# Gate projections in block products of four, rotary tables on another engine, and a reordered merge, in a hybrid diffusion layer

## The chip, the cores and the metric

The kernel runs on one core of one Trainium2 chip. The core has a matrix engine (PE, with its weight loads shown as PEld), a vector engine (DVE), an activation engine (ACT), a general engine (POOL) and a queue engine that issues most transfers (SP). The metric is the device time of one execution in microseconds (us); a lower time is better. Times are medians of several runs; the profile is one more execution, taken by the hardware profiler.

## The reference

One layer over 1024 latent tokens of width 1024 with 256 context tokens. Cut to what matters:

```python
m_lat = (silu(c) @ w_mod + b_mod).reshape(1, 1, 6, 1024)           # modulation rows
h_lat = rms_norm(x, norm_mix) * (1 + m_lat[:, :, 1]) + m_lat[:, :, 0]
aq, ak, av, bq, bk, bv, cq, cf, cb, ci, cg, gates = features(h_lat, w_in, ...)  # h_lat @ w_in, norms, rotary
yc = hgrn2_bidir(cq, cf, cb, ci, cg, ...)          # branch 2, linear recurrence in both directions
ya = window_attn(aq, ak, av, ctx k, ctx v, sink)   # branch 0, 8 heads, 2 key heads
yb = global_attn(bq, bk, bv, ctx k, ctx v)         # branch 1
up = einsum('blnw,nwd->blnd', stack(ya, yb, yc), w_branch)
x_mix = x + m_lat[:, :, 2] * (sum_n(sigmoid(gates) * up) @ w_out)
h = rms_norm(x_mix, norm_ffn) * (1 + m_lat[:, :, 4]) + m_lat[:, :, 3]
x = x_mix + m_lat[:, :, 5] * conv_ffn(h, ...)
return rms_norm(x, norm_final)
```

The gates are 3072 of the input projection's columns: for each of three branches eight tiles of 128 channels, 24 gate tiles in all.

## The kernel before

All products run with each fp32 operand split into a high part (a cast by ACT) and a low part (the difference, by DVE), and three matmuls for each pair: high by high, high by low, low by high. Everything lies with 128 partitions; the hidden state is `hh`, `hl`, each 128 x 8 x 1024.

The stages follow each other in this order: modulation rows 0 and 1, context and norm; the HGRN branch by four heads (`hgrn_head`); the stage between (lines 628 to 850); window attention (branch 0) and global attention (branch 1), both through `attention`; the merge (`merge_up`) and output projection (`wo_half`); the ConvFFN.

The framework places the instructions of each engine by a simulated run: an instruction has a priority from its place in the program, `tc.high_priority(offset=n)` moves it n places ahead, and among what is ready the first goes. Each engine then works through its own list in order, SP's list of transfers too. A tile comes from a pool with a fixed number of buffers for each tag; a new tile waits until a buffer of that tag is released.

The 24 gate tiles are listed in `gates` (line 612) as pairs (branch, tile) in the branch order 2, 0, 1. Before the change they are computed in four ways:

- `gates[0]` fills gaps of the last HGRN head (line 622), `gates[1:4]` are plain (`plain_gates`, line 689). A plain gate (`gate_unit`, line 564) takes 2 halves x 8 k x 3 = 48 matmuls of 512 columns; each half is drained by ACT (line 580) and stored by SP (line 581).
- `gates[4:10]` go in three pairs (`gate_pair`, line 738) through the scheme in `pair` (line 697): a 2 x 2 block product with seven multiplications in place of eight. One block side is the weights of two units by halves of the contraction, the other the hidden state by halves of the contraction and of the tokens.
- `gates[10:17]` are filler for the matrix engine in the first attention and `gates[17:24]` in the second (lines 853 to 859); `attention` spreads their steps over its iterations.

The block products need four sums of hidden-state blocks, T1 to T4 (`ht`, made by `h_sums`, line 654): DVE adds high and low parts into whole tiles (line 661), subtracts them (line 666), ACT casts and DVE takes the difference (lines 633 and 634). In the program these sums are woven with the three plain gates (line 693). `ctile` gives the tiles with tag "c", five buffers, for whole sums and for results. Product q uses block S_ORDER[q] (line 695): (0,0), T1, T2, (1,1), T3, (1,0), T4. Its weights come from one or two loads, a DVE sum (line 711) and a split (`w_split`), at a priority 100 places ahead; the results are drained by ACT copies or DVE sums.

The token projections (q, k, v of both attentions) go through the same scheme in three pairs (`tok_pair`, line 803). They use two two-bank tiles in PSUM, `za` and `zb`, in turn, and two single banks for product 5. A gate pair uses the two banks of one tile in turn and one single bank. After a token pair's product its results get a head norm (for branch 1) and the rotary step; these pieces wait in the list `behind`, and after every region of a later product one piece is put in. The rotary tables `tbq` and `tbk` are made once by POOL (line 684).

Token pairs and gate pairs alternate (lines 846 to 848).

In `attention` the result of an iteration is stored to `y_d` by SP (line 1640), each store after the iteration's last DVE operation.

`merge_up` (line 1751) goes through the branches in the order 2, 0, 1. For each it loads four tiles y from `y_d` (line 1761), splits them (lines 1762 and 1763), and multiplies by eight tiles of `w_branch`; a gate tile is loaded, put through a sigmoid and multiplied on. Before each gate tile it takes one step of `mod_rest` (line 588), which computes the modulation rows 2 and 3: a step loads 128 rows of `w_mod` into the only buffer `wmr` and DVE adds them, scaled, onto `macc`. There are 18 steps and 24 places, so they start with the first tile of the first branch.

Of the kernel before, what the change touches and what calls it, by code (L numbers as in the profile page):

```python
# [18 lines left out]
P = 128  # L19
D = 1024  # L20
KT = D // P
L = 1024
# [24 lines left out]
SPRIO = 40  # L47
TILED = 2
# [37 lines left out]
def build(tc, ins, out):  # L86
    nc = tc.nc
    V, A, G, T, SP = nc.vector, nc.scalar, nc.gpsimd, nc.tensor, nc.sync
    with ExitStack() as top:
# [522 lines left out]
        gates = [(n, i) for n in (2, 0, 1) for i in range(KT)]  # L612

# [30 lines left out]
        with ExitStack() as sp3:  # L644
# [9 lines left out]
            def h_sums():  # L654

                for k in range(0, KQ, 2):
                    ks = slice(k, k + 2)
                    f = {}
                    for a, b in ((0, 0), (0, 1), (1, 1), (1, 0)):
                        f[a, b] = ctile(f"h{a}{b}{k}")  # L660
                        V.tensor_tensor(out=f[a, b], in0=hb[a, b][0][:, ks].bitcast(F32),
                                        in1=hb[a, b][1][:, ks].bitcast(F32), op=add_)
                        yield

                    def put(n, out, x, y):
                        V.tensor_tensor(out=out, in0=x, in1=y, op=sub)
                        split([p[:, ks] for p in ht[n]], out)

                    put(1, f[0, 0], f[0, 1], f[0, 0])
                    yield  # L670
                    put(3, f[0, 1], f[1, 1], f[0, 1])
                    yield
                    put(2, f[1, 1], f[1, 1], f[0, 0])
                    yield
                    put(4, f[1, 0], f[1, 0], f[1, 1])
                    yield

# [3 lines left out]
            for nm, g in (("q", qnb), ("k", knb)):  # L681
                tb = p3.tile([P, LT, 2, 2, 32], F32, tag=f"tb{nm}", name=f"tb{nm}", bufs=1)
                for r in range(2):
                    G.tensor_tensor(out=tb[:, :, :, r], in0=cs,
                                    in1=g[:, None, None, r * 32:(r + 1) * 32].to_broadcast([P, LT, 2, 32]),
                                    op=ALU.mult)
                tabs[nm] = tb

            def plain_gates():
                for n, i in gates[1:4]:  # L690
                    yield from gate_unit(p3, n, i, "mm", ctile(f"g{n}{i}"))

            weave((plain_gates(), 48), (h_sums(), 16))

            S_ORDER = ((0, 0), 1, 2, (1, 1), 3, (1, 0), 4)

            def pair(nm, W, n, regions, unit, drains, behind):

                def load(t, i, j):
                    SP.dma_start(t, W(i, j))  # L700
                    return t

                def raw(i, j):
                    cnt[0] += 1
                    t = wp.tile([P, 1024], F32, tag="wr", name=f"wr{cnt[0]}", bufs=WR)[:, :KQ * n]
                    return load(t.rearrange("p (k n) -> p k n", k=KQ), i, j)

                s = p3.tile([P, 1024], F32, tag="s", name=f"s{nm}", bufs=1)[:, :KQ * n].rearrange("p (k n) -> p k n", k=KQ)
# [5 lines left out]
                for q in range(7):  # L714
                    with tc.high_priority(offset=wprio[0] + SPRIO):
# [13 lines left out]
                        w = w_split(src, KQ, n)  # L729
                    b = S_ORDER[q]  # L730
                    h = hb[b] if isinstance(b, tuple) else ht[b]
                    for x in range(len(regions(q))):
                        unit(regions(q)[x], w, h, x, q in (0, 1, 5))
                        for _ in range(1 if behind else 0):
                            behind.pop(0)()
                    drains(q)

            def gate_pair(g0, g1):

                nm = f"{g0[0]}{g0[1]}"  # L740
                idx = [U_C["gate"] + g[0] * 8 + g[1] for g in (g0, g1)]
                z = mm2(f"gp{nm}")
                zb = bank("b", f"gpb{nm}", (P, 512))
                cA, cB = ctile(f"gA{nm}"), ctile(f"gB{nm}")
                zq = lambda q: zb if q == 5 else z[:, q % 2 if q < 4 else 0]

                def unit(z, w, h, x, new):
                    wh, wl = w
                    hh_, hl_ = h
                    for k in (2 * x, 2 * x + 1):  # L750
                        on = dict(skip_group_check=True)
                        T.matmul(z, wh[:, k], hh_[:, k], start=new and k == 0, stop=False, **on)
                        T.matmul(z, wh[:, k], hl_[:, k], start=False, stop=False, **on)
# [1115 lines left out]
```

## Time and profile before

| | us |
|---|---|
| median of 3 runs | 2103.16 (2102.41 to 2103.4) |
| the profiled execution, device time | 2104.95 |
| its span, first to last instruction | 2103.2 |
| PE busy in it | 2028.2 |
| mean granted clock of PE, as a share of full | 0.99 |

A row of the timeline gives the start in us, the duration of one instruction (or of a row of them, with their count at the end), the engine, the line, the operation, output<-inputs by tile names, and in brackets how long the engine stood idle before it and what it waited for. A row of waits gives the waiting engine, tile and line, what it waited for, the sum in us, how many times, and the longest. A row of windows gives, for a stretch, the busy time and the count of each engine, the granted clock, the DMA share and GB/s. Durations of matmuls overlap, so their cost is read from start to start.

### The profile page before, as it was taken

What the parts mean: (1) busy time and instruction counts of PE and PEld (TensorE: products, weight loads), DVE (VectorE), ACT (ScalarE), POOL (GpSimd) and SP (SyncE); (2) the same over time, 40 slices, a digit from 0 to 9 for tenths busy, and PEclk for the clock granted to TensorE, in tenths of its full rate; (3) what the DMA queues carried; (4) which work ended last, traced back from release to release, by engine and by line L of the source; (5) the groups of instructions that cost most, each with busy time, mean ns of one, the idle gap of its engine ahead of it and who ended that gap; (6) DMA issues with size and microseconds to landing.
All of it is one profiled execution on the core that took longest, in us unless ns stands there. A gap on an engine that the chain in (4) does not pass through costs nothing. (4 is left out here: it accounts for less than half of the span.)

```text
span 2103.2 us, 29756 instructions
## 1 busy us (share of the span) xinstructions
PE 2028.2 (96%) x11321; PEld 1684.1 (80%) x11321; DVE 1521.3 (72%) x2440; ACT 1037.1 (49%) x1770; POOL 274.0 (13%) x245
## 2 busy tenths in 40 slices
PE   8999999989998999999999799999999999999997
PEld 5888888878996788788888577888888888888886
DVE  4846656686757788578887667888877777779964
ACT  3433333332233877688888633446445445544442
POOL 0000000021002232100000000010332343300001
PEclk9999999999999999999999999999999999999999
DMA  9311111133445211210110286592222222258722
GB/s 369 134 45 34 38 51 41 41 100 118 140 130 173 84 48 53 89 40 32 36 33 29 75 271 226 182 310 92 93 87 83 78 87 83 81 211 313 267 69 81
DMA packets 105023, 239.19 MB, mean 114 GB/s; under 512 B 10288, under 2 KB 35248, under 8 KB 103856
## 3 DMA queue, kind: packets, MB, share of 16 engines
q1 hardware_dynamic: 104880, 237.29, 33.8%
q8 instruction: 89, 1.46, 0.3%
q14 instruction: 54, 0.44, 0.1%
HBM read 191.64 MB, written 45.61 MB: 113 GB/s over the span
## 5 line engine op out<-in xcount | busy, mean ns | idle before, releaser
L1622 DVE TENSOR_TENSOR pl<-pp,ph 128x512 fp32r<-128x512 f32 x236 | 159.5, 687 | 31.8 <-ACT ph L1621 26.3
L166 ACT CAST wh<-wr 128x1024 fp32r<-128x1024 f32 x73 | 76.7, 1051 | 196.9 <-PE wo L191 34.4
L167 DVE TENSOR_TENSOR wl<-wr,wh 128x1024 fp32r<-128x1024 f32 x73 | 91.6, 1254 | 84.9 <-ACT wh L166 83.4
L1621 ACT CAST ph<-pp 128x512 fp32r<-128x512 f32 x236 | 135.6, 585 | 34.7 <-PE pp L1617 32.1
L190 PE MATMUL gz<-hh,wh 128*128 128x512 f32 x288 | 117.8, 410 | 8.4 <-ACT cg L580 6.9
L1209 PE MATMUL dn<-ac,wh 128*128 128x512 f32 (+2 forms) x311 | 119.3, 384 | 1.3 <-DVE xt L1217 1.2
L1210 PE MATMUL dn<-ac,wh 128*128 128x512 f32 (+2 forms) x311 | 119.3, 383 | 0.5 <-DVE ac L634 0.5
L1211 PE MATMUL dn<-ac,wl 128*128 128x512 f32 (+2 forms) x311 | 119.2, 383 | 0.0
L192 PE MATMUL gz<-hh,wl 128*128 128x512 f32 x288 | 114.9, 399 | 1.1 <-DVE wl L167 1.1
L191 PE MATMUL gz<-hl,wh 128*128 128x512 f32 x288 | 114.7, 398 | 0.0
L1603 PE MATMUL po<-ph,VHL 128*128 128x512 f32 x236 | 106.1, 450 | 1.9 <-ACT ph L1621 1.3
L1604 PE MATMUL po<-pl,VHL 128*128 128x512 f32 x236 | 97.9, 415 | 0.3 <-DVE pl L1622 0.2
L190 PE MATMUL br<-yh,wh 128*128 128x512 f32 x192 | 76.3, 399 | 11.2 <-ACT yh L1762 11.0
L191 PE MATMUL br<-yl,wh 128*128 128x512 f32 x192 | 76.5, 399 | 2.0 <-DVE yl L1763 1.9
L633 ACT CAST wh<-wr 128x1024 fp32r<-128x1024 f32 (+1 forms) x42 | 37.6, 897 | 82.2 <-PE tmt L826 22.5
L1617 PE MATMUL pp<-ident,plat 128*128 128x128 f32 x512 | 76.6, 273 | 0.3 <-DVE pl L1622 0.2
L1617 PEld LDWEIGHTS pp<-ident,plat 128*128 128x128 f32 x512 | 62.5, 140 | 17.6 <-DVE pl L1622 2.3
L956 ACT ACTIVATE u<-c,cw 128x1024 f32<-128x1024 f32 x38 | 47.3, 1246 | 58.0 <-DVE c L1111 30.0
L192 PE MATMUL br<-yh,wl 128*128 128x512 f32 x192 | 75.6, 395 | 0.0
L634 DVE TENSOR_TENSOR wl<-wr,wh 128x1024 fp32r<-128x1024 f32 (+1 forms) x42 | 43.1, 1029 | 44.7 <-ACT wh L633 44.7
L190 PEld LDWEIGHTS gz<-hh,wh 128*128 128x128 f32 x288 | 54.9, 191 | 18.0 <-ACT cg L580 7.6
L1209 PEld LDWEIGHTS dn<-ac,wh 128*128 128x128 f32 x311 | 58.4, 188 | 13.1 <-DVE xt L1217 1.0
(1531 smaller groups left out, 6316.6 us busy)
## 6 DMA issues: line engine op xcount, KB each, us to landing
wr<-in_w_up SPq DMA_DIRECT2D x44, 512.0 KB, 3.6
wr<-in_w_cm SPq DMA_DIRECT2D x42, 512.0 KB, 3.7
wmr<-in_w_mod SPq DMA_DIRECT2D x32, 512.0 KB, 5.0
wr<-in_w_dn SPq DMA_DIRECT2D x30, 512.0 KB, 4.3
b<-act_d SPq DMA_DIRECT2D x25, 512.0 KB, 5.8
sgt<-gate_d SPq DMA_DIRECT2D x24, 512.0 KB, 4.6
wr<-in_w_tm SPq DMA_DIRECT2D x23, 512.0 KB, 3.7
act_d<-u SPq DMA_DIRECT2D x22, 512.0 KB, 2.6
```

The lines of the kernel that those rows point to most:

```text
L167: (lo_eng or V).tensor_tensor(out=lo[:, :n], in0=raw[:, :n], in1=hi[:, :n].bitcast(F32), op=ALU.subtract)
L190: T.matmul(psl, wh[:, k, c], hh[:, k0 + k, cols], start=s, stop=False)
L191: T.matmul(psl, wh[:, k, c], hl[:, k0 + k, cols], start=False, stop=False)
L192: T.matmul(psl, wl[:, k, c], hh[:, k0 + k, cols], start=False, stop=e)
L1209: T.matmul(z, w[0][:, c], h[0], start=s, stop=False, **on)
L1210: T.matmul(z, w[0][:, c], h[1], start=False, stop=False, **on)
L1211: T.matmul(z, w[1][:, c], h[0], start=False, stop=e, **on)
L1603: T.matmul(po, vv, ph, start=n == 0, stop=False)
L1604: T.matmul(po, vv, pl, start=False, stop=n == len(kts) - 1)
L1617: T.transpose(pp[:, h], PT(h, n), ident)
L1621: A.copy(ph, pp)
L1622: V.tensor_tensor(out=pl, in0=pp, in1=ph.bitcast(F32), op=ALU.subtract)
```

## The change

It changes five things.

1. `gates.insert(2, gates.pop())` moves the last gate, (1, 7), to place 2. Two gates, `gates[1]` and `gates[2]`, are plain. Eight, `gates[3:11]`, go in two groups of four (`gate_group`), each after a token pair; the first two token pairs follow each other. The attentions have 7 and 6 gates as filler.
2. A group's weights are two gates side by side, so a tile is 128 x 4 x 256 and comes by two transfers of 256 KB whose pieces are 512 bytes. A group uses two two-bank tiles in turn and two single banks, 24 matmuls of 512 columns a product. Up to four pieces of `behind` are put in after each product of either kind.
3. `h_sums` comes in the program behind both plain gates, all of T1 first, and the rotary tables behind it, made by DVE.
4. The modulation steps are left out of the first branch of the merge; the tiles 0 and 4 of the other two take two steps. The loads and splits of the first branch's y get priority `YPRIO` = 100.
5. The last two stores of the second attention go through POOL's queue.

```diff
+YPRIO = 100
...
         gates = [(n, i) for n in (2, 0, 1) for i in range(KT)]
+        gates.insert(2, gates.pop())
...
+                def whole(a, b, k):
+                    f[a, b, k] = ctile(f"h{a}{b}{k}")
...
                 for k in range(0, KQ, 2):
...
+                    whole(0, 0, k)
+                    whole(0, 1, k)
+                    t = f[0, 0, k]
+                    put(1, t, f[0, 1, k], t, k)
+                for k in range(0, KQ, 2):
+                    b, t = f[0, 1, k], f[0, 0, k]
+                    whole(1, 1, k)
+                    put(3, b, f[1, 1, k], b, k)
+                    put(2, t, f[1, 1, k], t, k)
+                    whole(1, 0, k)
+                    put(4, t, f[1, 0, k], t, k)
+            for x in (1, 2):
+                for _ in gate_unit(p3, *gates[x], "mm", ctile(f"g{x}")):
+                    pass
+            h_sums()
...
-                    G.tensor_tensor(out=tb[:, :, :, r], in0=cs,
+                    V.tensor_tensor(out=tb[:, :, :, r], in0=cs,
...
-            weave((plain_gates(), 48), (h_sums(), 16))
...
                 def load(t, i, j):
-                    SP.dma_start(t, W(i, j))
+                    ws = W(i, j)
+                    n = 256 // len(ws)
+                    for x, w in enumerate(ws):
+                        SP.dma_start(t[:, :, x * n:(x + 1) * n], w)
                     return t
...
-                        for _ in range(1 if behind else 0):
-                            behind.pop(0)()
+                        for _ in range(4 // len(regions(q))):
+                            if behind:
+                                behind.pop(0)()
...
-            def gate_pair(g0, g1):
+            def gate_group(gs):
...
+                z = [mm2(f"{nm}{x}") for x in range(2)]
...
+                def regions(q):
+                    if q == 5:
+                        if not zc:
+                            zc.extend(bank("ab"[x], f"{nm}c{x}", (P, 512)) for x in range(2))
+                        return zc
+                    z_ = z[q % 2 if q < 4 else 0]
+                    return [z_[:, x] for x in range(2)]
                 def unit(z, w, h, x, new):
...
+                    cs_ = slice(x * P, (x + 1) * P)
+                    for k in range(KQ):
+                        T.matmul(z, w[0][:, k, cs_], h[0][:, k], start=new and k == 0, stop=False, **on)
+                        T.matmul(z, w[0][:, k, cs_], h[1][:, k], start=False, stop=False, **on)
+                        T.matmul(z, w[1][:, k, cs_], h[0][:, k], start=False, stop=k == KQ - 1, **on)
...
+                    if q >= 3:
+                        n, i = gs[(int(x[0]) - 1) * 2]
+                        SP.dma_start(gate_d[n, i:i + 2, :, (t1, t2)[int(x[1]) - 1]].rearrange("i p t -> p i t"), c[x])
...
-            for x, (a, b) in enumerate((((0, 2), (1, 2)), ((0, 0), (0, 1)), ((1, 0), (1, 1)))):
-                tok_pair(a, b)
-                gate_pair(*gates[4 + 2 * x:6 + 2 * x])
+            tok_pair((0, 2), (1, 2))
+            tok_pair((0, 0), (0, 1))
+            gate_group(gates[3:7])
+            tok_pair((1, 0), (1, 1))
+            gate_group(gates[7:11])
...
-        SP.dma_start(y_d[br].rearrange("k p t -> p k t")[:, 2 * g:2 * g + 2, tt * P:(tt + 1) * P], yT)
+        (G if br and it >= n_it - 2 else SP).dma_start(y_d[br].rearrange("k p t -> p k t")[:, 2 * g:2 * g + 2, tt * P:(tt + 1) * P], yT)
...
+            with tc.high_priority(offset=0 if j else YPRIO):
+                y = mp.tile([P, L], F32, tag="y", name=f"y{n}{k}")
+                SP.dma_start(y, y_d[n, k])
+                A.copy(yh[:, 0], y)
+                V.tensor_tensor(out=yl[:, 0], in0=y, in1=yh[:, 0].bitcast(F32), op=ALU.subtract)
...
-                next(mr, None)
+                if j:
+                    next(mr, None)
+                    if i % 4 == 0:
+                        next(mr, None)
```

More of the change, by code (lines that the diff above doesn't have):

```diff
@@ L733, in pair @@
                         unit(regions(q)[x], w, h, x, q in (0, 1, 5))
-                        for _ in range(1 if behind else 0):
-                            behind.pop(0)()
+                        for _ in range(4 // len(regions(q))):
+                            if behind:
+                                behind.pop(0)()
                     drains(q)
-            def gate_pair(g0, g1):
[L740 to L745, printed above, removed]
-                def unit(z, w, h, x, new):
[L748 to L753, printed above, removed]
-                        T.matmul(z, wl[:, k], hh_[:, k], start=False, stop=k == KQ - 1, **on)
@@ L756, in drains @@
                 def drains(q):
[L757 removed]
+                    x = OUT[q]
+                    if x not in c:
+                        c[x] = ctile(f"{nm}{x}")
+                    z_ = z[q % 2 if q < 4 else 0]
                     if q in (0, 1, 2, 6):
[L759 to L762 removed]
@@ L763, in drains @@
-                    if q >= 5:
-                        n, i = (g0, g1)[q - 5]
-                        SP.dma_start(gate_d[n, i], (cA, cB)[q - 5].rearrange("p a b -> p (a b)"))
-                pair(nm, lambda i, j: ins["w_cm"][idx[i]].rearrange("p (k n) -> p k n", n=P)[:, j * KQ:(j + 1) * KQ], P,
-                     lambda q: [zq(q)] * 2, unit, drains, behind)
+                        A.copy(c[x], z_)
+                    elif q == 5:
+                        for y in range(2):
+                            V.tensor_tensor(out=c[x][:, y], in0=zc[y], in1=c[x][:, y], op=add_)
+                    else:
+                        V.tensor_tensor(out=c[x], in0=z_, in1=c[x], op=add_)
@@ L770, in rope, with W @@
+                    if q >= 3:
+                        n, i = gs[(int(x[0]) - 1) * 2]
+                        SP.dma_start(gate_d[n, i:i + 2, :, (t1, t2)[int(x[1]) - 1]].rearrange("i p t -> p i t"), c[x])
+                def W(i, j):
+                    return [ins["w_cm"][U_C["gate"] + n * 8 + g].rearrange("p (k n) -> p k n", n=P)[:, j * KQ:(j + 1) * KQ]
+                            for n, g in gs[2 * i:2 * i + 2]]
+                pair(nm, W, regions, unit, drains, behind)
             def rope(x, nh, tt, tab, nm):
@@ L828, in drains @@
                 def drains(q):
[L829 removed]
+                    x = OUT[q]
                     if x not in c:
```

64 lines of the change are left out of this document (24 added, 40 removed).

## The prediction, made before the changed kernel was run

> **What bounds the kernel now.** I read the head of the page, then the list of PE's waits, then the stages by windows, and last the timelines of the places where PE stands idle.
>
> ```profile
> span 2103.2 us, 29756 instructions
> PE 2028.2 (96%) x11321; PEld 1684.1 (80%) x11321; DVE 1521.3 (72%) x2440; ACT 1037.1 (49%) x1770; POOL 274.0 (13%) x245
> ...
> PE br L190 <- ACT yh L1762: 11.0, 4, 8.9
> PE gp L752 <- ACT cgA L759: 9.9, 4, 4.7
> PE gz L190 <- ACT cg L580: 6.9, 2, 6.8
> PE gp L752 <- ACT cgB L759: 2.7, 3, 1.0
> PE br L191 <- DVE yl L1763: 1.9, 3, 1.1
> PE tmt L824 <- DVE ct L838: 0.3, 1, 0.3
> ```
>
> TensorE bounds it: 2028 of 2103 us. So a change can win in two ways: fewer matmuls, or less of the 75 us in which PE stands. Of those 75 the list puts 12.9 on the first pass of the merge (br), 12.6 on the gate pairs (gp), 6.9 on a plain gate (gz), and only 0.3 on the three token pairs (tmt), which use the same seven products.
>
> ```profile
> 428.90:442.70 13.80, 7.06 (x32) 5.47 (x30) 13.80 (x10) 3.52 (x4) 8.84 (x4) 0.89 0.43 133
> 442.70:461.80 19.10, 18.89 (x78) 15.47 (x79) 19.10 (x18) 7.95 (x10) 0.00 (x0) 0.90 0.24 84
> 501.70:528.40 26.70, 21.67 (x86) 16.43 (x85) 17.80 (x61) 8.49 (x15) 2.75 (x4) 0.94 0.58 177
> 636.00:667.00 31.00, 22.84 (x76) 16.46 (x77) 27.02 (x82) 9.96 (x18) 10.52 (x9) 0.83 0.39 119
> 1195.40:1213.60 18.20, 7.04 (x20) 4.25 (x20) 6.42 (x8) 7.25 (x8) 0.00 (x0) 0.72 0.72 241
> ```
>
> After the length come PE, PEld, DVE, ACT, POOL, then the granted clock. An idle stretch is paid twice: the clock falls to 0.72 to 0.94 around it. The timeline shows both prices:
>
> ```profile
> 443.32 0.63 PE L191 MATMUL gz<-hl,wh 128*128 128x512 f32 x1
> 443.75 0.63 PE L192 MATMUL gz<-hh,wl 128*128 128x512 f32 x1
> ...
> 1341.16 0.39 PE L192 MATMUL br<-yh,wl 128*128 128x512 f32 x1
> ...
> 1346.60 0.39 PE L192 MATMUL br<-yh,wl 128*128 128x512 f32 x1
> ```
>
> A 128x512 matmul costs (1346.60 - 1341.16) / 24 = 0.227 us from start to start (their 0.39 overlaps), and 0.43 (443.32 to 443.75) behind the 6.8 us idle stretch.
>
> **Part 1: matmuls.** A plain gate takes 48 matmuls of 512 columns; a block product of a group of four takes 24, so its seven products take 168, 42 a gate, the same as in the pairs of before (84 for two). Eight gates instead of six in blocks: 2 x 6 x 0.227 = **2.7 us** less. The gate moved to the front costs there what it saves as filler of the second attention.
>
> **Part 2: groups for pairs.** Why pairs stall and token pairs do not:
>
> ```profile
> 508.18 0.79 PE L752 MATMUL gp<-T1h,wh 128*128 128x512 f32 x1 [3.58 <-ACT cgA L759]
> ...
> 501.89 0.62 ACT L633 CAST wh<-s 128x512 fp32r<-128x512 f32 x1 [5.14 <-PE tmt L826]
> 506.63 0.51 ACT L1340 ACTIVATE hsq<-ct 128x128 f32<-128x128 f32 x2 [2.66 <-DVE hrs L1343]
> 507.55 0.57 ACT L759 COPY cgA<-gp 128x512 f32<-128x512 f32 x1
> ```
>
> Product T1 goes to the second bank of the tile that product 0 filled, and PE starts it only after ACT has copied out the first bank (507.55 + 0.57 = 508.1), though its weights were cast at 501.9. ACT is late since it sits in a head norm of the token pair before, which waits for DVE. A pair's product is 12 matmuls, 2.7 us, so nothing covers this. The group takes two separate tiles in turn, as token pairs do; a tile comes round again after a whole other product of 24 x 0.227 = 5.4 us, more than the 3.6 or 4.7 us that ACT is late. So I price it by the token pairs' 0.3, not by the pairs: 12.6 us of waits go, and clock of (1 - 0.94) x 26.7 + (1 - 0.83) x 31.0 = 6.9. Bounds for what is left: 0, and all 19.5. The first products still carry eight rotary steps of the token pair, four per product instead of two; I leave 4 for that: **-15.5 us**. Casts, weight sums and drains get tiles of 1024 instead of 512 and become 14 sets in place of 21; the token pairs run with that size already.
>
> The loads change form: each 512 KB comes as two transfers in 512-byte pieces. The nearest row is a store of such pieces; these lines are the answer for the 3.5 us around one:
>
> ```profile
> DMA packets 272, 0.13 MB, mean 37 GB/s; under 512 B 16, under 2 KB 272, under 8 KB 272
> q1 hardware_dynamic: 272, 0.13, 13.2%
> ...
> wr<-in_w_cm SPq DMA_DIRECT2D x42, 512.0 KB, 3.7
> wr<-in_w_cm SPq DMA_DIRECT2D x21, 256.0 KB, 2.8
> q1 hardware_dynamic: 104880, 237.29, 33.8%
> ```
>
> 0.132 x 16 x 3.5 / 272 = 27 ns a packet; 1024 pieces on 16 engines take 1.7 us. Eight loads per seven products leave 5.4 x 7 / 8 = 4.8 us for each, so nothing waits: 0. The other end is the whole run's mean packet, 0.338 x 16 x 2103.2 / 104880 = 108 ns (rival 4). A load has a fixed part: 512 KB lands in 3.7 us and 256 KB in 2.8, which leaves 1.9 that doesn't shrink. If the two halves stood one behind the other, a load would take 5.6 instead of the 4.8 us there is for it, 16 x 0.8 = 13 us more. [...] I take 0, since both halves are issued together and well ahead, so that their fixed parts can overlap.
>
> **Part 3: sums and tables.** Why the plain gate stalled:
>
> ```profile
> 428.91 4.62 DVE L661 TENSOR_TENSOR ch<-hh,hl 128x1024 f32<-128x1024 f32 x4
> 437.90 2.28 DVE L666 TENSOR_TENSOR ch<-ch,ch 128x1024 f32<-128x1024 f32 x1
> ...
> 432.46 4.43 POOL L684 TENSOR_TENSOR tbq<-cs,qnb 128x512 f32<-128x512 f32 x2 [5.75 <-DMA cs<-in_rope]
> ...
> L824 PE MATMUL tmt<-wh,T2h x48: 283/283/283, 472.9 to 608.4; 128*128 128x256 f32 x48
> ...
> 497.85 0.28 PE L825 MATMUL tmt<-wl,T4h 128*128 128x256 f32 x1
> 497.97 0.28 PE L826 MATMUL tmt<-wh,T4l 128*128 128x256 f32 x1
> ```
>
> While POOL makes the tables a DVE sum takes 2.28 instead of 1.14 us (4.62 / 4). DVE fell behind, ACT's cast of a sum waited, and the gate's drain stood behind that cast. On DVE the four tables, half as long as a sum, cost some 4 x 0.6 = 2.4 us, off PE's path, and ahead of the rotary steps that need them by two products. With both gates ahead of the sums the 6.8 us wait goes, and (1 - 0.90) x 19.1 = 1.9 of clock: 8.7. What is late next is T2. PE came to its product at 472.9; one plain gate less (10.9) and 8.7 less bring that to 453.3. DVE starts at 428.9 and has 21 sum steps and about 6 weight steps ahead of T2's last part: 27 x 1.14 = 30.8, so 459.7, or some 464 if the sums wait for a "c" tile (five tiles, two of them held by the gates until stored). That gap of 6 to 11 us can be filled: the product (1,1) needs no sum and lasts 48 x 0.12 = 5.8 (497.85 to 497.97 is one of its size). I take 5 us of it as left (ends 0 and 11, plus about 2 of clock): **-4 us**.
>
> **Part 4: start of the merge.**
>
> ```profile
> 1179.93 0.39 PE L192 MATMUL gz<-hh,wl 128*128 128x512 f32 x1
> 1194.99 0.49 PE L1604 MATMUL po<-pl,VHL 128*128 128x512 f32 x1 [0.23 <-DVE pl L1622]
> 1204.37 1.22 PE L190 MATMUL br<-yh,wh 128*128 128x512 f32 x2 [8.89 <-ACT yh L1762]
> ...
> 1186.14 11.92 SPq L1640 DMA_DIRECT2D y_d<-yT  x2
> 1198.16 0.91 SPq L1761 DMA_DIRECT2D y<-y_d  x2
> ```
>
> SP stands in the last attention store until 1198, and the loads of y, finished since the HGRN stage, are behind it. On POOL the two stores hold nobody: what they write is read two passes later. The memory of y is that of hh and hl, whose last reader here is PE at 1180, so four loads and splits fit ahead of 1195. From 1195.4 to 1213.6 PE did 20 matmuls, 4.5 us of work; 13.7 were lost. One is left for the added casts at the tail: **-12.7 us**.
>
> **Part 5: modulation rows.** Moved out of the first pass, their 16 steps fall on the two later ones.
>
> ```profile
> DVE macc L598 <- DMA wmr<-in_w_mod: 24.8, 15, 3.2
> 1301.40:1346.80 45.40, 44.87 (x193) 36.55 (x194) 37.02 (x54) 20.38 (x26) 0.00 (x0) 0.96 0.49 159
> ```
>
> The second pass already runs eight such steps. The third, the row shown, would take eight more at about 1.2: DVE 37.0 + 9.6 = 46.6 in 45.4. That is the edge, not over it, as steps that are ready can run in the first pass all the same; **+1 us**, ends 0 and +14 (rival 3).
>
> **Part 6: second attention**, with six filler gates instead of seven.
>
> ```profile
> 900.00:1000.00 100.00, 99.36 (x579) 80.47 (x577) 80.41 (x137) 83.69 (x183) 2.40 (x6) 1.00 0.11 35
> ```
>
> PE is full, DVE and ACT above 80%. Of the 10.9 us that leave I count on 9: **+2**, ends 0 and +10.9.
>
> **Sum:** -2.7 - 15.5 - 4 - 12.7 + 1 + 2 = -31.9. The profiled execution took 2104.95, 1.8 above the median of the runs, 2103.16; 2104.95 - 31.9 = 2073.0, and as a median **2071 us**.
>
> **Rivals.** (1) T2 late in full: the gap stays 11 and costs 2 of clock, +8: 2079. For it: five "c" tiles. Against it: PE's order leaves program order where something else is ready. (2) The change doesn't do what it says at the merge: y's loads are still placed after the last store's data, since memory or the planner's order holds them; +12: 2083. For it: in the trace of before nothing of the merge is loaded ahead of 1198 although hh was free at 1180. Against it: SP was blocked there. (3) The rows bind the third pass: DVE, in order, stands before each of the eight rows for the 24.8 / 15 = 1.65 us above: 37.0 + 8 x (1.2 + 1.65) = 59.8 against 45.4 of the pass, +14 in place of +1: 2084. Against it: the more DVE has to do, the less it waits for a load that is already under way. (4) The other side: the weight stream binds the groups. At 108 ns a piece a load takes 64 x 0.108 = 6.9 us of every engine, and a group with its four 512 KB stores (another 6.9) 62 against 38 us of PE work: 2 x 24 = 48, hence 2119, slower. It begins to cost at 61 ns and eats the whole gain at about 92. Against it: the measured 27 ns. Halves that stand one behind the other are the milder form, +13: 2084. (5) The second attention doesn't shorten, bound by ACT and DVE: +9: 2080. Against it: PE is at 99.4% there.
>
> **Chances.** Forecast 0.56; it going better in all parts, down to 2104.95 - 1.8 - (2.7 + 19.5 + 8.7 + 13.7) = 2058, belongs to it. Rival 1 0.10, rival 2 0.11, rival 3 0.08, rival 5 0.08, rival 4 0.03 and its milder form 0.02; 0.02 for no gain at all. About 0.2% is what a measurement of this kernel tells from no change. Only rival 4 is slower: 0.03; same 0.02; faster 0.95. The range takes in rivals 1, 2, 3, 5 and the milder form, with a margin of 4 us for two of them at half size, and reaches down to all parts at their best: 2057 to 2088.
>
> **What would show it.** In the profile after: waits of the groups' tiles on ACT under 5 us in all; 128x1024 DVE sums all at 1.14 and no POOL work before the head norms; y's loads issued before 1190 and no br wait above 1; the third pass no longer than 46 us. Wrong would be: PE waits on T2 above 8, tmt or group products waiting for a weight DMA, br still waiting on yh, or sgt and xm steps of the third pass behind macc.

## The result, and the profile after

The changed kernel takes 2079.34 us, the median of 4 runs (2076.56 to 2079.69); before, 2103.28 in the runs beside it. The ratio is 0.9882, 95% interval 0.9865 to 0.9899: faster by 24.8 us, 21 to 28 (the two medians alone differ by 23.9). The forecast was 2071 with a range of 2057 to 2088. The profiled execution went from a span of 2103.2 to 2077.2. One of the four runs of experiment 11 below was slow (3373 us, at a granted clock of 0.57 where the others had 0.99), and the median given there counts it; its other three lie at 2077.6 to 2079.3. First the head of the profile after, then PE's waits (engine, line, tile, what it waited for: us in total, times, longest):

```profile
span 2077.2 us, 29706 instructions
PE 2019.9 (97%) x11309; PEld 1679.6 (81%) x11309; DVE 1519.3 (73%) x2430; ACT 1033.9 (50%) x1753; POOL 273.0 (13%) x243
```
```profile
PE tmt L846 <- ACT ct L855: 8.2, 1, 8.2
PE br L191 <- ACT yh L1790: 4.5, 3, 1.9
PE g L768 <- DVE wl L636: 3.5, 2, 1.7
PE br L192 <- DVE yl L1791: 1.7, 4, 0.5
PE g L766 <- ACT wh L635: 1.0, 1, 1.0
```

The matmuls fell by 12, as counted. The waits of the gate pairs (gp) and of the plain gate (gz) are gone; a wait of 8.2 us that did not exist stands in the first token pair, at the product of T2. Five stages by windows (length; then PE, PEld, DVE, ACT, POOL busy and their instructions; then the clock): T2's product, the two gate groups, the start of the merge, its third pass.

```profile
452.40:465.00 12.60, 4.44 (x25) 4.23 (x25) 12.60 (x12) 4.96 (x5) 0.00 (x0) 0.73 0.00 0
531.40:570.00 38.60, 38.60 (x174) 32.03 (x174) 27.44 (x49) 11.55 (x12) 0.00 (x0) 1.00 0.65 203
617.50:655.00 37.50, 32.84 (x133) 25.77 (x134) 32.58 (x76) 12.40 (x16) 14.11 (x9) 0.95 0.44 137
1175.40:1192.20 16.80, 11.38 (x32) 7.39 (x32) 7.88 (x9) 9.94 (x11) 0.74 (x1) 0.80 0.55 193
1275.00:1320.60 45.60, 44.63 (x201) 36.53 (x200) 43.68 (x60) 20.89 (x27) 0.00 (x0) 1.00 0.70 230
```

I call *lost* what a stretch is longer than its matmuls need, at the 0.227 us (512 columns) and 0.12 us (256 columns) that the prediction took from the trace. T2's stretch holds 25 matmuls of 256 columns, 3.0 us in 12.6: 9.6 lost. The first group has 168 of 512 and 6 of 256 and loses nothing; the second, 133 x 0.227 = 30.2 in 37.5, loses 7.3. The start of the merge loses 16.8 - 32 x 0.227 = 9.5. In the trace of before the sums lost 27.0 - 82 x 0.227 = 8.4:

```profile
428.40:455.40 27.00, 20.22 (x82) 16.25 (x81) 27.00 (x21) 8.13 (x10) 8.84 (x4) 0.87 0.36 117
```

The three pairs of before lost 7.3 + 3.4 + 13.7 = 24.4 by the same reckoning (good to some 0.5 us each, as a window cuts matmuls at its ends), the start of the merge 13.7.

The 26.0 us of span came from here (last products, first scores and first output projection are the marks):

| stretch | before | after | change | matmuls |
|---|---|---|---|---|
| up to the sums | 428.4 | 428.1 | -0.3 | same |
| sums, token pairs, gates | 268.9 | 254.7 | -14.2 | +19 of 512 columns |
| both attentions | 497.7 | 492.2 | -5.5 | 31 fewer |
| merge | 151.8 | 145.8 | -6.0 | same |
| rest | 756.4 | 756.4 | 0 | same |

### The profile page after: what moved, and what is told of

Read it like the earlier page. It is cut to its first block, busy times and chain, and to the rows that moved or that the text cites. A ratio compares the mean times of both kernels' runs of the same rounds, so it can differ in the third digit from the quotient of the medians.

```text
span 2077.2 us, 29706 instructions
## 1 busy us (share of the span) xinstructions
PE 2019.9 (97%) x11309; PEld 1679.6 (81%) x11309; DVE 1519.3 (73%) x2430; ACT 1033.9 (50%) x1753; POOL 273.0 (13%) x243
## 3 DMA queue, kind: packets, MB, share of 16 engines
q1 hardware_dynamic: 118224, 238.08, 34.3%
## 4 chain that ended last, share of the span: by engine, by line
PE 65%; DVE 7%; DMA 3%; ACT 2%; POOL 1%; issue 1%; SPq 0%; DVEq 0%; POOLq 0%; ACTq 0%
PE pp L1644 4%; PE dn L1236 3%; PE dn L1238 3%; PE dn L1237 3%; PE up L1101 3%; PE up L1103 2%; PE up L1102 2%; PE po L1630 2%; PE po L1631 2%; PE gz L192 2%; PE gz L191 2%; PE gz L193 2%; PE upc L1103 2%; PE upc L1102 2%; PE upc L1101 2%; PE upd L1103 2%
## 5 line engine op out<-in xcount | busy, mean ns | idle before, releaser
L191 PE MATMUL gz<-hh,wh 128*128 128x512 f32 x256 | 104.0, 406 | 0.5 <-ACT gs L581 0.5
L193 PE MATMUL gz<-hh,wl 128*128 128x512 f32 x256 | 102.5, 400 | 0.0
L192 PE MATMUL gz<-hl,wh 128*128 128x512 f32 x256 | 101.5, 397 | 0.0
L1236 PEld LDWEIGHTS dn<-ac,wh 128*128 128x128 f32 x311 | 58.4, 188 | 12.9 <-DVE xt L1244 1.0
L1237 PEld LDWEIGHTS dn<-ac,wh 128*128 128x128 f32 x311 | 58.4, 188 | 12.3 <-DVE ac L636 1.0
```

Source lines behind the costliest of these rows:

```text
L191: T.matmul(psl, wh[:, k, c], hh[:, k0 + k, cols], start=s, stop=False)
L192: T.matmul(psl, wh[:, k, c], hl[:, k0 + k, cols], start=False, stop=False)
L193: T.matmul(psl, wl[:, k, c], hh[:, k0 + k, cols], start=False, stop=e)
L1236: T.matmul(z, w[0][:, c], h[0], start=s, stop=False, **on)
L1237: T.matmul(z, w[0][:, c], h[1], start=False, stop=False, **on)
```

## Experiments

Each is a run of its own with its profile; "the changed kernel" is the one above. Medians within some 3 us of each other can't be told apart (the intervals of the ratios are 0.15% wide on each side), so small effects are read from their stage of the profile, not from the total.

### 1. The start of the merge: y without tiles of its own

```diff
-                y = mp.tile([P, L], F32, tag="y", name=f"y{n}{k}")
+                y = yl[:, 0].bitcast(F32)
                 SP.dma_start(y, y_d[n, k])
```

> The merge's y has no tile of its own any more: it is loaded into the tile of its low part, and the subtraction is made in place; the rest is the changed kernel (span 2077.2, median 2079.3). Theory (two y buffers hold the loads): in the changed kernel loads 3 and 4 leave SP at 1178.8 and 1184.9, behind the subtractions of loads 1 and 2. With four loads under way at once, the casts come before the last product of the attention, PE loses at the start of the merge 2 us or less instead of 9.5: 2070 to 2073, br waiting for yh under 1 us. Rival (the casts stand behind the attention's casts on ACT, wherever the loads are): the first br still starts 2 us after the last product and only the two later gaps go, at most 5 us: 2074 to 2078.

In the changed kernel the two y tiles hold up the later loads (timeline, SP's issues and ACT's casts; the second number is the duration, and an issue that waits for a buffer is long):

```profile
1164.94 0.86 SPq L1789 DMA_DIRECT2D y<-y_d  x2
1178.84 1.45 SPq L1789 DMA_DIRECT2D y<-y_d  x2
```
```profile
1176.29 1.99 ACT L1790 CAST yh<-y 128x1024 fp32r<-128x1024 f32 x2
1185.90 1.05 ACT L1790 CAST yh<-y 128x1024 fp32r<-128x1024 f32 x1 [2.25 <-DMA y<-y_d]
```

So the stores on POOL did free SP: the first two loads leave at 1165. But their casts stand behind the attention's last copies on ACT, and loads 3 and 4 wait for the subtractions that follow these casts (they leave at 1178.84 and 1179.97; the load at 1184.9, which the expectation takes for the fourth, is the second branch's). With y in place all loads left at 1159 and the first br came at 1164.3. Measured: 2078.94 (0.9883, 0.9868 to 0.9898), no gain. The profile of this run, SP, ACT and PE:

```profile
1165.70 20.52 SPq L595 DMA_DIRECT2D wmr<-in_w_mod  x3
```
```profile
1194.74 1.06 ACT L1807 ACTIVATE sgt<-sgt 128x1024 f32<-128x1024 f32 x1 [9.45 <-DMA sgt<-gate_d]
```
```profile
1188.75 0.77 PE L191 MATMUL br<-yh,wh 128*128 128x512 f32 x1 [4.31 <-DVE xm L1810]
```

Both theories fall: neither the two tiles nor the casts' place is what costs the time in the end. The products that came early pushed the attention's last product from 1175.0 to 1182.4. Then SP stood 20.5 us in three loads of modulation rows, whose one buffer waits for DVE, with the gates' loads behind it; and the third output waited 4.3 us for an accumulator, which DVE frees with the step xm. The output projection started at the same time as in the changed kernel.

### 2. The last stores back on SP

```diff
-        (G if br and it >= n_it - 2 else SP).dma_start(y_d[br]...
+        SP.dma_start(y_d[br]...
```

> The last two attention stores are issued by SP again, the rest is the changed kernel. Theory (SP standing in these stores is what held the loads of y): the loads leave after the last store again, the first br comes some 9 us after the last product, and what the start of the merge has won is lost: 4 us, 2083 to 2084. Rival (the loads were placed earlier by their raised priority, and the queue of the stores is beside the point): 2079, with the loads issued at 1165 as now.

2083.06 (0.9903, 0.9889 to 0.9918): 4.1 slower than run 1 beside it, 3.7 than the changed kernel. From the last product of the attention to the output projection it took 149.4 us instead of 145.8. SP's issues:

```profile
1167.56 11.74 SPq L1667 DMA_DIRECT2D y_d<-yT  x2
1179.39 0.91 SPq L1789 DMA_DIRECT2D y<-y_d  x2
```

SP stands 11.7 us in the two stores, and the loads follow the last one. The queue was the reason, as the theory had it, and the stores on POOL are worth some 3.6 us. The raised priority of these loads does nothing: with `YPRIO` = 0 the program comes out the same, instruction for instruction.

### 3. The modulation rows in the first pass again

```diff
-                if j:
-                    next(mr, None)
-                    if i % 4 == 0:
-                        next(mr, None)
+                next(mr, None)
```

> The modulation rows are made in passes one to three of the merge again, one to an output, the rest is the changed kernel. Theory (the place of the rows costs and brings nothing, DVE is not the bound in any pass): 2079, within 1. Rival (moving them won something: the third pass of before ran at a clock of 0.96, that of after at 1.00): 1.5 to 3 slower, 2081 to 2082, with the loss in passes one and three.

2078.16 (0.9878, 0.9863 to 0.9892); from the attention's last product to the output projection 144.3 us. The place of the rows makes no difference that can be measured, as the theory said.

### 4. T2 and T3 ahead of T4

```diff
                 for k in range(0, KQ, 2):
                     b, t = f[0, 1, k], f[0, 0, k]
                     whole(1, 1, k)
-                    put(3, b, f[1, 1, k], b, k)
                     put(2, t, f[1, 1, k], t, k)
-                    whole(1, 0, k)
-                    put(4, t, f[1, 0, k], t, k)
+                    put(3, b, f[1, 1, k], b, k)
+                for k in range(0, KQ, 2):
+                    whole(1, 0, k); put(4, f[0, 0, k], f[1, 0, k], f[0, 0, k], k)
```

> In the sums, both halves of T2 and T3 come before T4 (three DVE steps of T4 and two of T3 no longer stand ahead of T2's last part); the rest is the changed kernel. Theory A (PE waits for T2, which DVE delivers at 462.1): T2 comes 5.7 us earlier, the gap of 8.2 us shrinks to about 3 and with it the clock loss: 5 to 6 faster, 2073 to 2074. Theory B (PE waits for the copy of product 0 out of its tile, which takes one of the five c tiles that the sums hold, and stands on ACT behind a cast of T4): T2 is early, the copy still starts after the first T4 cast, some 2 us earlier than now: 1 to 3 faster, 2076 to 2078, and PE starts T2's product within 0.2 us of the copy's end.

First the changed kernel at the wait: DVE's splits, ACT's queue, PE's matmuls.

```profile
458.64 1.22 DVE L636 TENSOR_TENSOR T4l<-ch,T4h 128x1024 fp32r<-128x1024 f32 x1
460.91 1.22 DVE L636 TENSOR_TENSOR T2l<-ch,T2h 128x1024 fp32r<-128x1024 f32 x1
```
```profile
456.49 1.05 ACT L635 CAST T4h<-ch 128x1024 fp32r<-128x1024 f32 x1 [4.57 <-DVE ch L667]
458.76 1.05 ACT L635 CAST T2h<-ch 128x1024 fp32r<-128x1024 f32 x1
459.71 1.92 ACT L855 COPY ct<-tmt 128x1024 f32<-128x1024 f32 x2
```
```profile
460.77 0.58 PE L846 MATMUL tmt<-wh,T2h 128*128 128x256 f32 x1 [8.16 <-ACT ct L855]
461.15 0.42 PE L847 MATMUL tmt<-wl,T2h 128*128 128x256 f32 x1
461.37 0.41 PE L848 MATMUL tmt<-wh,T2l 128*128 128x256 f32 x1
...
464.28 0.28 PE L847 MATMUL tmt<-wl,T2h 128*128 128x256 f32 x1
464.40 0.28 PE L848 MATMUL tmt<-wh,T2l 128*128 128x256 f32 x1
```

PE starts T2's product at 460.77, right behind the first of the two copies that begin at 459.71, and before the last split of T2 (460.91 + 1.22) is there. Product 0 was finished at 446.7; its copy stood on ACT behind casts of T4, T3 and T2, the first of which waited 4.57 us for DVE. In this run:

```profile
460.86 1.21 DVE L636 TENSOR_TENSOR T2l<-ch,T2h 128x1024 fp32r<-128x1024 f32 x1
```
```profile
461.93 1.00 ACT L855 COPY ct<-tmt 128x1024 f32<-128x1024 f32 x1
```
```profile
462.99 0.58 PE L846 MATMUL tmt<-wh,T2h 128*128 128x256 f32 x1 [8.49 <-ACT ct L855]
```

2079.75 (0.9884, 0.9867 to 0.9900), and the wait is 8.5 us as before (this execution was 2 us behind at the start of the sums already). T2 was complete at 462.07; PE started at 462.99, behind the end of the copy (461.93 + 1.00). So the copy binds, as theory B had it, but the 1 to 3 us that it forecast didn't come: with T2 only 0.9 us ahead of the copy, both have to move.

### 5. T4's sums behind the first products

As run 4, and in place of its second loop:

```diff
+                def t4(k):
+                    whole(1, 0, k)
+                    put(4, f[0, 0, k], f[1, 0, k], f[0, 0, k], k)
+                return [lambda: None] * 8 + [lambda: t4(0), lambda: t4(2)]
...
-            behind = []
+            behind = t4s
```

> As the run before with T2 and T3 ahead of T4, and T4's own sums and splits are taken out of the block of sums and put among the units of the third product of the first token pair, so that two c tiles come free before the copies of products 0 and 1. The rest is the changed kernel. In the run before, PE's wait stayed at 8.5 us, and T2's product started 0.1 us behind the end of the copy, though T2 itself was there before. Theory B (the copy out of the tile, queued on ACT behind the casts of T3 and T4, is what PE waits for, and T2 is some 1 to 6 us behind it): with both out of the way the wait falls from 8.2 to 8.5 us to between 2 and 4, with its share of clock 4 to 7 us faster than the changed kernel: 2072 to 2075, span 2070 to 2073. Theory A (only T2 counts, and DVE has nothing else to leave out): wait of 6 or more, gain 2 at most.

2075.98 (0.9869, 0.9854 to 0.9884), span 2072.5, 4.7 less than the changed kernel's. The 8.2 us broke into three:

```profile
453.32 1.01 ACT L855 COPY ct<-tmt 128x1024 f32<-128x1024 f32 x1 [1.16 <-DVE T3l L636]
```
```profile
454.38 0.38 PE L846 MATMUL tmt<-wh,T2h 128*128 128x256 f32 x1 [1.68 <-ACT ct L855]
457.82 0.58 PE L846 MATMUL tmt<-wh,T2h 128*128 128x256 f32 x1 [2.47 <-ACT T2h L635]
459.87 0.58 PE L846 MATMUL tmt<-wh,hh 128*128 128x256 f32 x1 [1.25 <-ACT ct L855]
```

Copy, T2's second half, and the copy of product 1 end within 5.5 us of each other. That is what theory B expected, with 5.4 instead of 2 to 4 us left; the middle one, a cast that waits for DVE's sum, shows DVE's work ahead of T2 as a next bound. The row of ACT shows what else holds the copy of product 0: it starts when DVE has finished T3's split (453.28), the step that gives up a c tile. So the copy waits for a tile, and not for its place in the queue alone.

### 6. The rotary steps spread in the second group

```diff
-                        for _ in range(4 // len(regions(q))):
+                        for _ in range(1):
```

> One rotary step behind each unit of a product everywhere: two instead of four behind a product of a gate group, so the steps left over from a token pair lie beside four products instead of two. The rest is the changed kernel. Theory (ACT and DVE stand in head norms at the second group, and its weights are cast and split late): the waits of the second group (5.2 us of g and g26c on wl and wh) fall under 1.5 and the stretch of 37.5 us with 133 matmuls goes to 32 to 33: 4 to 6 faster, 2073 to 2075. Rival (the weight sums or their loads are late by themselves): the waits stay where they are within 1 us, 2078 to 2080.

2076.48 (0.9871, 0.9849 to 0.9893). The time lies between the two forecasts, and the waits of the group stayed, as the rival had it: 5.2 us on wl. Spreading the steps was no remedy. The changed kernel, 612 to 652, by windows and by DVE's waits:

```profile
612.00:652.00 40.00, 34.74 (x142) 27.03 (x141) 34.51 (x90) 13.03 (x19) 15.12 (x10) 0.96 0.38 114
```
```profile
DVE ct L814 <- POOL hrs L1372: 5.5, 10, 0.9
```

DVE worked 34.5 us and stood 5.5 in the chain of the head norm (square on ACT, sums on DVE, power on POOL, product on DVE): 40.0 of 40.0. In run 6 it is 34.3 + 5.6 = 39.9: DVE's stretch is full either way, so spreading its steps inside the group changes nothing. That DVE binds here is read from this sum; no run took its work away.

### 7. The kernel before, with two tiles for a pair

```diff
-                z = mm2(f"gp{nm}")
+                z = [mm2(f"gp{nm}{x}") for x in range(2)]
...
-                zq = lambda q: zb if q == 5 else z[:, q % 2 if q < 4 else 0]
+                zq = lambda q: zb if q == 5 else z[q % 2 if q < 4 else 0][:, 0]
```

> The kernel before, with its pairs of gates, but the products 0 and 1 of a pair go to two tiles, each with one bank in use, instead of the two banks of one tile. Nothing else changes. Theory (the shared tile makes PE wait for ACT's copy; a product of 2.7 us covers only a part of ACT's lateness): PE's waits of gp on ACT fall from 12.6 us to between 3 and 6, the three pairs lose 12 to 16 us instead of 24.4: 2089 to 2095 against 2103. Rival 1 (tiles alone are the cause, the length of a product is not): the waits go below 1, the pairs lose 5 or less, 2080 to 2084. Rival 2 (ACT's lateness comes out in any case, at the next product): waits stay above 9, 2098 to 2103.

2099.35 (0.9982, 0.9972 to 0.9991), 3.9 faster than before. Waits of PE:

```profile
PE gz L192 <- DVE wl L167: 7.8, 1, 7.8
PE gp L752 <- DVE cgB L762: 3.3, 1, 3.3
```

The waits on the copies cgA and cgB on ACT fell from 12.6 to 0.9, and the second pair lost nothing (3.4 before). But the first pair lost some 7 us as before, 3.3 of it now at its last product and for DVE, and the third pair and the stretch behind it lost 18.0 us where they had lost 15.7: 7.8 of it in a plain gate whose weights DVE had not split. Rival 2 has the time right and the engine wrong: the lateness comes out at later products, but on DVE. That fits a full DVE, as in run 6. In the trace of before, its windows and DVE's waits from 620 to 667:

```profile
620.00:667.00 47.00, 37.78 (x188) 30.41 (x188) 39.93 (x125) 13.10 (x25) 16.42 (x15) 0.89 0.31 96
```
```profile
DVE ct L792 <- POOL hrs L1345: 8.0, 13, 1.1
```

It was busy for 39.9 us and waited 8.0 for POOL, 47.9 of 47 (the first of these waits, 1.1 us, ended just ahead of the window).

### 8. y in place, and the rows loaded by POOL

As run 1, and the loads of the modulation rows in the merge are issued by POOL.

> As the run with y in place, and the loads of the modulation rows in the merge are issued by POOL instead of SP. With y in place the first br came at 1164, 18 us before the last product of the attention, but SP then stood 20.5 us in loads of modulation rows (one buffer, which waits for DVE), with the branch weights and the gates' loads behind them, and PE lost the gain again. Theory (SP's queue is what took the gain): SP is free, gates and weights come in time, the merge loses 3 us or less in all: 6 to 9 faster than the changed kernel, 2070 to 2073. Rival (the gates' loads and the outputs' tiles come late for another reason, memory that the attention still holds, or ACT and DVE are full at the end of the attention): PE waits 4 us or more on xm or yh all the same, 2076 to 2080.

2085.39 (0.9914, 0.9899 to 0.9929), 6 slower than the changed kernel: the theory falls. SP no longer stood in the rows, and stood instead in the next loads that had to wait for a buffer, branch weights and gates:

```profile
1169.88 25.70 SPq L164 DMA_DIRECT2D wr<-in_w_branch  x2
1196.50 16.69 SPq L1806 DMA_DIRECT2D sgt<-gate_d  x4
```

PE waited 5.6 us for xm, which is the rival's sign, though the time is worse than the rival's too, and 4.7 for yl, which on DVE stood behind a modulation row not yet loaded. The last product of the attention slipped to 1189.2. Starting the merge earlier, beside an attention that keeps ACT and DVE busy, gained nothing in either run.

### 9. The last rotary steps behind the second group

```diff
-            gate_group(gates[7:11])
-            while behind:
+            late, behind[:] = behind[:], []; gate_group(gates[7:11])
+            while behind.extend(late) or late.clear() or behind:
```

> The rotary and head-norm steps that are left of the last token pair when the second gate group begins are put behind that group instead of into its first two products (their tiles hold q of the second attention, which is read 200 us later). The rest is the changed kernel. Spreading the steps over four products moved the waits and kept their sum, and in the stretch 612 to 652 DVE was busy for 34.5 us and stood another 5.5 in waits for POOL's part of the head norm: 40.0 of 40. Theory (DVE, not the drains and not the loads, binds the second group): its 133 matmuls take 31 to 33 us instead of 37.5, the waits on wl and wh go below 1, and DVE does the steps in the 28 us before the first attention, of which it fills 8.6: 4 to 6 faster, span 2071 to 2073. Rival (the steps delay the lead-in of the first attention by as much): the group is faster and the next stretch longer, 2077 to 2080.

2077.87 (0.9882, 0.9867 to 0.9897). The waits of the group fell from 5.2 to 3.7 us, and the lead-in of the first attention waited 2.5 us for ACT (kt on qs_kk, 0.4 before): lost from 617.5 to the first scores 4.1 + 2.8 = 6.9 against 7.3 + 0.5. Mostly moved, as the rival had it. DVE was still busy for 35.1 of the 40 us from 612 to 652 and waited another 4.8 for POOL, in 7 waits instead of 10: most of the steps were still done there, so this run doesn't show what the group takes without them.

### 10. The tables on POOL

```diff
-                    V.tensor_tensor(out=tb[:, :, :, r], in0=cs,
+                    G.tensor_tensor(out=tb[:, :, :, r], in0=cs,
```

> The four rotary tables are made by POOL again, the rest is the changed kernel. Theory (POOL's table work halves DVE's rate while it runs): POOL works some 9 us from 436 on, DVE's sums beside it take up to 2.3 instead of 1.14 us, DVE loses 4 and saves 2.4; T2 and the copy before it come 1 to 3 us later, PE's wait on ct is 9 to 11 instead of 8.2, 1 to 3 slower. Rival (what slowed the sums of before was something else, a transfer or the plain gates): the sums stay at 1.14, the wait falls to 6, 2 faster.

2082.40 (0.9907, 0.9893 to 0.9922), some 3 slower, and PE's wait on ct is 10.5 us. DVE and POOL:

```profile
435.58 3.87 POOL L693 TENSOR_TENSOR tbq<-cs,qnb 128x512 f32<-128x512 f32 x2 [9.44 <-PE gz L193]
439.40 4.52 POOL L693 TENSOR_TENSOR tbk<-cs,knb 128x512 f32<-128x512 f32 x2
```
```profile
434.83 1.22 DVE L667 TENSOR_TENSOR ch<-ch,ch 128x1024 f32<-128x1024 f32 x1
...
440.45 2.32 DVE L636 TENSOR_TENSOR T1l<-ch,T1h 128x1024 fp32r<-128x1024 f32 x1
442.69 2.31 DVE L663 TENSOR_TENSOR ch<-hh,hl 128x1024 f32<-128x1024 f32 x1
...
446.06 1.21 DVE L667 TENSOR_TENSOR ch<-ch,ch 128x1024 f32<-128x1024 f32 x1
```

While POOL works (435.6 to 443.9) a step of DVE with two operands takes 2.0 to 2.3 us, before and behind it 1.2. The Trainium skill (GPSIMD Engine Reference, Specifications) gives a reason: POOL shares its way to SBUF, the memory on the chip, with VectorE (DVE) and contends with its instructions that read two inputs there. The trace agrees and gives the size: little more than half the rate.

### 11. A third plain gate ahead

```diff
-        gates.insert(2, gates.pop())
+        gates[2:2] = [gates.pop(), gates.pop()]
...
-            for x in (1, 2):
+            for x in (1, 2, 3):
...
-            gate_group(gates[3:7])
+            gate_group(gates[4:8])
```

(the second group and the start of the fillers move by one in the same way)

> A third plain gate is computed ahead of the token pairs (three instead of two beside the sums; two gates instead of one are taken from the end of the list), and the second attention has five filler gates instead of six. The number of matmuls is that of the changed kernel. Theory (PE's wait at T2 is a matter of cover: DVE and ACT need until 460.8 whatever PE does): PE comes to T2's product 10.9 us later and waits no more, the 9.6 us lost there are gone; the second attention gives back 9 of 10.9: in all 6 to 9 faster, 2070 to 2073. Rival 1 (a third gate with its c tile and its two drains pushes the sums back by as much, since five c tiles bind): the wait stays above 5, gain under 4. Rival 2 (the second attention doesn't get shorter by this gate): the wait is gone, 2078 to 2081.

2078.64 (0.9887, 0.9867 to 0.9907). PE came to T2's product 11 us later and still waited 8.4 us. Rival 1 of the expectation, the c tiles, is what came. DVE:

```profile
433.82 1.22 DVE L717 TENSOR_TENSOR st<-st,wr 128x1024 f32<-128x1024 f32 x1 [5.24 <-DMA gate_d<-cg]
...
445.54 3.49 DVE L663 TENSOR_TENSOR ch<-hh,hl 128x1024 f32<-128x1024 f32 x3
```

The first three sums (ch) ran at 428.6 in the changed kernel. Here, where three gates hold three of the five c tiles, they run at 445.5, and DVE, with no sum to work on, stands idle for 5.2 us. Run 12 takes the gates out of these tiles and has the three sums back at 428.7; its other edits come behind them, so the tiles were the reason. The second attention gave back nearly all of its gate: both attentions took 482.0 us instead of 492.2.

### 12. Cover, and free tiles

Runs 5, 9 and 11 together, and the three plain gates are drained into the memory that T4 gets later:

```diff
+            gst = [hs_.tile([P, KQ, LH], F32, tag=f"T4{p}", name=f"G4{p}") for p in "hl"]
...
-                for _ in gate_unit(p3, *gates[x], "mm", ctile(f"g{x}")):
+                for _ in gate_unit(p3, *gates[x], "mm", gst[x // 3][:, x % 3 // 2 * 2:x % 3 // 2 * 2 + 2]): pass
+            ht[4] = [hs_.tile([P, KQ, LH], F32R, tag=f"T4{p}", name=f"T4{p}") for p in "hl"]
```

> The changed kernel with what the runs point to: three plain gates ahead, drained into the memory that T4's two tiles get later, so that the gates hold none of the five c tiles; T2 and T3 before T4, and T4's sums among the units of the third product; the last rotary steps behind the second gate group. With the third gate alone PE's wait at T2 stayed at 8.4 us, since the sums began 17 us later, behind the stores of the gates that held the tiles. Theory (the c tiles, shared by gates, sums and drains, are what sets the time of the copies and of T2; with them free DVE needs until about 458, and PE comes to T2 at 463): PE's wait at T2 is under 1.5, the 9.6 us lost there are gone, the second attention takes one gate less at no loss, the second group wins 3: 9 to 13 faster than the changed kernel, 2066 to 2070, span 2064 to 2068. Rival (DVE's work until T2, 24 to 27 steps of 1.14 us and the weights' between them, binds by itself, whatever the tiles): a wait of 4 us or more stays, 2071 to 2075.

2069.06, median of 5 (2066.02 to 2071.08); ratio 0.9840, 0.9826 to 0.9853, clear of the changed kernel's interval; span 2064.2. T2's stretch, and DVE's first three sums and its last split of T2:

```profile
463.50:477.00 13.50, 13.50 (x115) 13.50 (x114) 10.12 (x10) 6.87 (x7) 0.00 (x0) 1.00 0.45 146
```
```profile
428.72 3.49 DVE L663 TENSOR_TENSOR ch<-hh,hl 128x1024 f32<-128x1024 f32 x3
...
453.30 1.22 DVE L636 TENSOR_TENSOR T2l<-ch,T2h 128x1024 fp32r<-128x1024 f32 x1
```

There is no wait at T2 any more; the 115 matmuls of the stretch (115 x 0.12 = 13.8) fill it. The sums start at 428.7 again, with three gates ahead of the token pairs, and T2 is complete at 454.5 instead of 462.1. This is the fastest version of the study, 10 us below the changed kernel. It joins four edits, and what each brings of the 10 us was not separated.

## Why the prediction came out as it did

The time lies inside the range. The sum was -31.9 against -26.0 between the two profiles, and its parts did not all come in as named. Two of the signs that the prediction set for being wrong came: a wait above 8 us at T2's product, and br still waiting on yh.

**Part 1**, -2.7: 12 matmuls fewer, exactly as counted.

**Part 2**, -15.5: measured -17.1 (24.4 lost before, 7.3 after). The size was near, by luck in part; the reason was not right. The prediction held the shared tile and ACT's late copy responsible. Run 7 took the sharing away and won 3.9 us; the loss reappeared at later products. What binds there, as far as the rows tell, is DVE with the rotary steps and head norms of the token pair (40.0 of 40 us in the changed kernel, 47.9 of 47 before). A group would then win because it lays 38 us of matmuls beside the same DVE work where a pair laid 19, which no run shows by itself; the first group, beside steps without a head norm, loses nothing, and the second still loses 7.3. The "4 left" was undersized by 3.3; that the pairs had lost 4.9 more than the 19.5 us which the prediction counted made up for it. The weight pieces cost nothing: no product waited for a DMA, and the packets of 512 bytes in the changed kernel's trace take 28 ns in the mean, where the prediction had 27. Two halves of 256 KB issued together land in 3.6 us each, about what one load of 512 KB took (the first group's stretch, median from issue to landing):

```profile
wr<-in_w_cm SPq DMA_DIRECT2D x4, 256.0 KB, 3.6
```

One behind the other they would take 5.6 us by the prediction's figures. Their fixed parts overlap, so that rival 4 and its milder form are out. (From its own terms, 9 x 64 pieces against 38 us, rival 4 would begin to cost at 66 ns a piece and eat the gain at about 94, not at 61 and 92; nothing hangs on it.)

**Part 3**, -4: measured +1.2 (8.4 lost before, 9.6 after). This step failed. The prediction saw T2 late and let PE fill some 6 of the 11 us with product (1,1); PE kept program order, and 9.6 us were lost where 5 were allowed. And it looked at T2 alone: what PE waited for was the copy of product 0, queued on ACT behind casts that wait for DVE's sums, and waiting for one of the five c tiles besides (runs 4, 5, 11, 12). That is rival 1, which had named the five tiles but not the copy; it was given a chance of 0.10. That its 2079 is also the measured total is chance, since Part 4 fell short as well. The tables were better on DVE, as priced: on POOL they cost some 3 us more (run 10). But their 2.4 us were not off PE's path: they stand in DVE's unbroken row of work ahead of T2 (435.7 to 441.5).

**Part 4**, -12.7: measured -4.2 at the start of the merge (13.7 lost before, 9.5 after), of which the stores on POOL brought 3.6 (run 2). The step that failed is "four loads and splits fit ahead of 1195": the loads left at 1165, but only two had tiles, and ACT's queue put the casts behind the attention's. Neither was the last bound (runs 1 and 8). Rival 2 had most of the size (8.5 us of its 12) and the cause wrong: the loads did advance.

**Part 5**, +1: nothing measurable in the total (run 3). In the third pass, one of the two into which the rows moved, PE waits for them once, behind macc, and otherwise stands idle for next to nothing (1275 to 1320.6, above):

```profile
PE pm L605 <- DVE macc L599: 1.0, 1, 1.0
```

That is the +1, and rival 3's 14 did not come. The merge behind its start took 1.8 less than before. **Part 6**, +2: the attentions shortened by 5.5 with 31 matmuls (7.0 us) fewer, so 1.5 were not given back; run 11 gave another gate back nearly in full (10.2 of 10.9). Rival 5 is out.

Together -2.7 - 17.1 + 1.2 - 4.2 - 1.8 + 1.5 = -23.1; the other 2.9 us of the difference, 2.6 of them between the sums and the first scores, were not traced further.

What stays open is what it would take to begin the merge without a loss: some 8 us remain in the fastest version too (the first 32 matmuls of the merge, 7.3 us of work, take the 15.2 us from 1165.4 to 1180.6), and runs 1 and 8 only moved them. Open is also what the second group takes with DVE's work out of its way.

## What to carry to other kernels

When an engine stalls, add up over the stretch, for every engine beside it, the busy time and the waits inside that engine's own chain, before blaming the tile named in the wait: an engine whose sum fills the stretch is the likely bound, and freeing the tile may only move the wait. When a stall goes, list all that is late next, with the queue that each stands in and the buffer that it needs: a copy behind casts on an in-order engine can be later than the data itself. And cover pays only if its own results don't take the buffers that the covered work needs: a third gate gained nothing until, in run 12, its output went elsewhere, together with the other edits of that run.

## What the runs showed of the hardware

A long wait costs TensorE (PE) more than its length. After the 8.2 us at T2 the matmuls of 256 columns followed each other at 0.21 us until 464.1 and at 0.12 from then on (the rows in run 4): 3.4 us at little more than half the rate, which is the 1.4 us between the 8.2 us waited and the 9.6 lost. Behind the 8.5 us wait of run 4 it took 4.0 us (462.99 to 466.99), behind the 4.3 us wait of run 1 3.3 us (1188.75 to 1192.0), so the price hardly follows the length of the wait. The Trainium skill (TensorE: Matmul & The Clock Gate, What's actually happening) puts it the same way: after an idle window the clock is halved until about 3.4 us of activity have passed. These three waits agree with the number.

An engine that is not the bottleneck by its share can bind a stretch in full: DVE was at 73% over the span and at 86% busy in the second group, and the missing 14% were its own waits for POOL inside one chain.
